# A unit's preparation queued behind the last unit's fourth inversion step, its inputs in one piece a partition, and other places for the first branch

## The chip, the core and the metric

One Trainium2 chip, one of its cores. The metric is the device time of one execution in microseconds, median over several runs. The core's engines run side by side, each in the order of its own instruction queue: TensorE (matrix products and transposes; "PE" in the profile, its weight loads "PEld"), VectorE ("DVE"), ScalarE ("ACT"), GpSimd ("POOL") and SyncE ("SP"), which here issues all data transfers (DMA) between the chip's DRAM and the on-chip memories. SBUF is the working memory with 128 partitions, PSUM the eight banks into which TensorE writes.

## The reference

One layer of a hybrid encoder on x (1024 tokens, 1024 channels), in float32:

```
h = x @ w_in                            # split into inputs of four branches
y_a = rglru(...)                        # linear recurrence with a short convolution
y_b = short_conv(...)                   # gated convolution over 3 tokens
y_c = rwkv7(...)                        # 8 heads of 64, a state of 64 x 64 per head
y_d = chunk_attention(q, k, v, bias)    # 8 heads, chunks of 64, band of 9 chunks
merged = sum over n of sigmoid(x @ w_gate[n] + b_gate[n]) * (y[n] @ w_branch[n])
x = layer_norm(ALPHA * x + merged @ w_out)
ff = square(relu(x @ w_ff1)) @ w_ff2
out = layer_norm(ALPHA * x + ff + (p @ w_ple) * sigmoid(x @ w_ple_gate + b))
```

The step of rwkv7, for each head and token: `sa = state @ a_t`, then `state = state * w_t + sa b_t^T + v_t k_t^T`, then `o_t = state @ r_t`, followed by a normalisation over the head, a bonus term and a gate.

## The kernel before

**Dense products.** A float32 product is made of three products of rounded parts (lines 362 to 364: high x high, high x low, low x high). Pairs of weight columns go through `seven`, a scheme with seven block products instead of eight; x stands on the chip for it as seven blocks, `11`, `21`, `N2`, `N1`, `T3`, `22`, `N4`, each as high and low parts of 512 columns (pool `xp`). A pair uses them in just this order. Results that a later stage needs go to DRAM. A piece is one of the seven products, 12 matmuls of 512 columns.

**Units of the third branch.** The class `Rwkv` handles the recurrence in sixteen units: two halves of the heads (`hf`), eight blocks of 128 tokens (`b`). Counted here from 0 to 15. A unit has these stages:

- Loads by SyncE: `zt` (lines 110 and 111: r, k, v and the two transformed low-rank terms, ten rows of 128 values a partition), `gg` (the gate), `vs` twice (v with its chunks exchanged). `zs` in DRAM holds them, written by `zc_done` (line 626) and `low_rank` (line 686) in pieces of 512 tokens.
- Preparation: ScalarE makes the decays from `zt` (lines 123 and 124), VectorE the running products (lines 128 to 132), the norm of `kk` goes through TensorE (line 147), then `ar`, `bk`, the matrix products of line 191, masked in line 195, transposes (lines 203 and 208) and, last, `YT` in line 221.
- Inversion of a triangular matrix by six doubling steps, `li` 0 to 5: `Yo` (line 237), a product (line 242), an addition (line 243), four transposes (line 227) and a copy by ScalarE (line 228). It ends with a correction (lines 248 to 255) and `TTf` (line 257). `mark` is the last matmul of line 255.
- The tail: two chunks one after the other through the state (lines 261 to 285), normalisation, and the store `ys` (line 308).

Many tiles have one place (`bk`, `wm`, `kk`, `km`, `I`), others two (`zt`, `gg`, `vs`, `ar`, `D`). Five of a unit's intermediate products share the two PSUM banks of tag `q`.

**Order.** Each engine's queue is set at build time by a planner that simulates the engines and takes, whenever one is free, the ready instruction that ranks first. Units are traced with `tc.high_priority(HP)`, HP = 3000, ahead of the dense pieces. After each unit the program traces ten pieces (twelve for the first four units), and from the fourth unit on these may come on TensorE only behind the `mark` of the unit two before (`tc.issue_after`, lines 755 to 758). What `issue_after` names is an instruction; all that the block traces on that instruction's engine is queued behind it.

**After the units.** The other dense pieces (the last are gate products), the attention and the recurrence and convolution branches (`lru`, `sconv`) run side by side (lines 993 to 999). Then `xp`, the temporaries `tx` and the weight buffers `wq` are closed (line 1003), and new pools take their space, in the order in which they are opened: `wfp`, `bp`, `tp`, `lt`. A tile of them waits for those old tiles that lay in its place. The branches are projected in the order 2, 1, 0, 3 (third branch first): four inputs `yf` are loaded and split into `yh` and `yl` (lines 1034 to 1039), at the places that `kind` names, `s1` and `s2` in `bp`, `s3` and `s4` in `lt`; then come the products `br` and the sums `acc` (`s3`).

Of the kernel before, what the change touches and what calls it, by code (L numbers as in the profile page):

```python
# [10 lines left out]
F32 = mybir.dt.float32  # L11
# [30 lines left out]

class Rwkv:


# [33 lines left out]
    def start_half(s, hf):  # L81
        for t in s.P:
            s.nc.gpsimd.memset(t, 0.0)
        s.ip = 0

    def unit(s, hf, b):
        nc, cst, ident = s.nc, s.cst, s.ident
        V, A, G, T, SY = nc.vector, nc.scalar, nc.gpsimd, nc.tensor, nc.sync
        u = f"_{hf}_{b}"
# [15 lines left out]
        def heads(x):  # L105
            return x.rearrange("p (h n) -> p h n", h=4)
# [1 line left out]

        tok = slice(b * 128, b * 128 + 128)
        zt = st("zt", [128, 10, 128])  # L110
        SY.dma_start(zt, s.zs[hf, 0:10, :, tok].rearrange("t p n -> p t n"))
        gg = st("gg", [128, 2, 128])
        SY.dma_start(gg, s.zs[hf, 10:12, :, tok].rearrange("t p n -> p t n"))
        vs = st("vs", [128, 2, 2, 64])
        for c in range(2):
            SY.dma_start(vs[:, :, 1 - c, :], s.zs[hf, 4:6, :, b * 128 + c * 64:b * 128 + c * 64 + 64].rearrange("t p n -> p t n"))
        r, k, v = zt[:, 0:2, :], zt[:, 2:4, :], zt[:, 4:6, :]


        tw = zt[:, 6:8, :].rearrange("p a (c n) -> p (a c) n", c=2)  # L120
# [103 lines left out]
        def transposed(dst, src, n):  # L224
            p = ps("pt")
            for h in range(4):
                T.transpose(p[:, h * 128:h * 128 + 128], src.bitcast(F32)[:, h, :], ident)  # L227
            A.activation(dst, heads(p), AF.Copy)  # L228

        transposed(Y, YT, 0)  # L230
        for li in range(6):
            z = 2 ** li
            n = 64 // z
            Yo = st("Yo", [128, 256], dt=F32R)
            yv = Y.rearrange("p h (n two s) -> p h n two s", two=2, s=z)[:, :, :, 0, :]
            lm = cst[:, C_LV + li * 64:C_LV + li * 64 + 64].rearrange("p (n s) -> p n s", s=z)[:, None].to_broadcast((128, 4, n, z))
            V.tensor_tensor(Yo.rearrange("p (h n s) -> p h n s", h=4, s=z), yv.bitcast(F32), lm, op=ALU.mult)
            if li == 5:
                V.tensor_tensor(Y, Y.bitcast(F32), ident[:, None, :].to_broadcast((128, 4, 128)), op=ALU.add)
            p1 = ps("py", 256)  # L240
            for h in range(4):
                T.matmul(p1[:, h * 64:(h + 1) * 64], YT[:, h, :], Yo[:, h * 64:(h + 1) * 64], start=True, stop=True)  # L242
            V.tensor_tensor(yv, yv.bitcast(F32), p1.rearrange("p (h n s) -> p h n s", h=4, s=z), op=ALU.add)  # L243
            YT = st("YT", [128, 4, 128], dt=F32R)
            transposed(YT, Y, 1 + li)
        Tn, TN = Y, YT
        pr = ps("py")
        T.matmul(heads(pr), s.idr, s.idr[:, None, :].to_broadcast((128, 4, 128)), start=True, stop=False)
# [119 lines left out]
def trunk(ctx, tc, xT, xn, pT, w_in, w_gate, w_branch, w_out, w_ff1, w_ff2, w_ple, w_pg,  # L368
# [25 lines left out]
        turn[tag] = turn.get(tag, -1) + 1  # L394
        return bank(banks[tag][turn[tag] % len(banks[tag])], name, w)

    zs = dr.tile([2, 12, 128, 1024], F32, name="zs")
    zw = dr.tile([128, 1024], F32, name="zw")
    qkv = dr.tile([3, 4, 128, 1024], F32, name="qkv")
    hd = dr.tile([20, 128, 1024], F32, name="hd")  # L400
# [118 lines left out]
    def part(name, k, which, dt=F32R, tile_name=None):  # L519
        return xp.tile([128, 512], dt, tag=f"x{name}{which}{k}", name=tile_name or f"x{name}{which}{k}")  # L520

    def xload(kb, j, k, t):
        SY.dma_start(t, xT[4 * kb + k][:, j * 512:j * 512 + 512])
        return t
# [81 lines left out]
    def xpair(w0, w1, name, done):  # L606

        nx[0] += 1
        return seven(XA, weights(w0, w1, name), name, done, tmp, nx[0] % 2, 1 - nx[0] % 2, late=False)

    def zc_done(i0, keep):

        ds, last = {}, {}

        def finish(i, j):
            t, d = i0 + i, ds.pop((i, j))
            if j:
                V.scalar_tensor_tensor(d[:, 0:1], last[i], mu[:, 0, t:t + 1], d[:, 0:1], op0=ALU.mult, op1=ALU.add)
            if t == 12:
                A.activation(d[0:64, :], d[0:64, :], AF.Tanh)  # L620
                SY.dma_start(zw[:, H[j]], d)
            elif t == 13:
                A.activation(d, d, AF.Tanh, scale=0.5)
                V.tensor_scalar(d, d, 0.5, 0.5, op0=ALU.mult, op1=ALU.add)
            else:
                SY.dma_start(zs[t % 4 // 2, t // 4 * 2 + t % 2][:, H[j]], d)

        def done(i, j, z, sign):
            t = i0 + i
            if sign:  # L630
                p, z = z, keep(f"z{t}{j}")
                A.activation(z, p, AF.Copy, scale=float(sign))
            if t == 13:
                sg.insert(j, rw("zt", "sg1", shape=(128, 1280))[:, 0:512] if j else rw("wm", "sg0"))
            ds[i, j] = d = sg[j and -1] if t == 13 else keep(f"zd{t}{j}")
            A.activation(d, z, AF.Copy, scale=mu[:, 1, t:t + 1])
            V.scalar_tensor_tensor(d[:, 1:512], z[:, 0:511], mu[:, 0, t:t + 1], d[:, 1:512], op0=ALU.mult, op1=ALU.add)
            if j == 0:
                last[i] = mx.tile([128, 1], F32, tag="zl", name=f"zl{t}", bufs=8)
                A.activation(last[i], z[:, 511:512], AF.Copy)  # L640
                finish(i, 0)
            if (i, 1) in ds and i in last:
                finish(i, 1)

        return done
# [6 lines left out]
    def low_rank(d):  # L652


        for kind in range(3):
# [9 lines left out]
            for h in range(2):  # L665
# [9 lines left out]
                for j in range(4):  # L675
                    cs = slice(j * 128, j * 128 + 128)
                    p = ps("q", f"gl{kind}{j}{h}")
                    t = rw("TTf" if j % 2 else "bh", f"lt{kind}{j}{h}", F32)
                    if kind < 2:
                        T.matmul(p, wh[:, cs], dh, start=True, stop=False)  # L680
                        T.matmul(p, wh[:, cs], dl, start=False, stop=True)
                        A.activation(t, p, AF.Tanh, scale=0.5, bias=hb[:, kind, j:j + 1])
                    else:
                        gm.acc(p, [(wh[:, cs], wl[:, cs], dh, dl)])
                        A.activation(t, p, AF.Copy)
                    SY.dma_start(zs[j // 2, 6 + 2 * kind + j % 2][:, sl], t)

    def to_dram(where):

# [60 lines left out]
    for hf in range(2):  # L750
        R.start_half(hf)
        for b in range(8):
            with tc.high_priority(HP):
                marks.append(R.unit(hf, b))
            with ExitStack() as after:
                if len(marks) > max(LAG, L0):
                    after.enter_context(tc.issue_after(marks[-1 - LAG]))
                run(NO if len(marks) > N0 else NOB)
# [245 lines left out]
    banks["g"] = [0, 1]  # L1004
    wf_ = ctx.enter_context(tc.tile_pool(name="wfp", bufs=2, reuse_waits="tile"))
    gm.wf = wf_
    bp = ctx.enter_context(tc.tile_pool(name="bp", bufs=1, reuse_waits="tile"))
    tp = ctx.enter_context(tc.tile_pool(name="tp", bufs=4, reuse_waits="tile"))
    lt = ctx.enter_context(tc.tile_pool(name="lt", bufs=1, reuse_waits="tile"))
    pools = {"s1": bp, "s2": bp, "s3": lt, "s4": lt}  # L1010

# [14 lines left out]
    for n in (2, 1, 0, 3):  # L1026
# [6 lines left out]
        for k in range(4):  # L1033
            yf = wf_.tile([128, 1024], F32, tag="wf", name=f"yf{n}{k}", bufs=2)
            SY.dma_start(yf, ysd[n][k])
            kind = ("s2", "s1", "s4", "s4")[n]
            yh = slot(kind, 2 * k, [128, 1024], F32R, f"yh{n}{k}")
            yl = slot(kind, 2 * k + 1, [128, 1024], F32R, f"yl{n}{k}")
            gm.split(yf, yh, yl)
# [341 lines left out]
```

## Time and profile before

| | |
|---|---|
| three runs, us | 2447.42, 2448.84, 2454.46 |
| median, us | 2448.84 |
| the profiled execution, us | 2449.66 |
| its span (first to last instruction), us | 2447.9 |
| mean granted TensorE clock, share of full speed | 0.96 |

The profile is of one execution. Its span is shorter than its time by what lies before the first and behind the last instruction. The clock of TensorE is granted at one of two levels, 2.4 GHz (1.00) or 1.2 GHz (0.50); a stretch that has both shows a mean. A matmul's busy time includes its pipeline, so a busy TensorE is not one at its peak.

### The profile page before, as it was taken

The numbers are of one execution on the slowest core, as the hardware profiler recorded it, in microseconds if no ns is written. First come the engines' busy times: TensorE is split into PE (matmuls) and PEld (weight loads), VectorE is DVE, ScalarE is ACT, GpSimd is POOL, SyncE is SP. The second block draws the span as 40 slices with busy tenths as digits, with TensorE's granted clock in tenths as the row PEclk, the third lists the DMA queues.
The fourth block names the chain that finished last, engine by engine and source line by source line (L and its number), as shares of the span: only waits on it lengthen the run. The fifth ranks groups of instructions, "written<-read, shape, count | busy, mean of one in ns | idle before, by whom it ended". The sixth has DMA issues, their size and how long they took to land.

```text
span 2447.9 us, 32202 instructions
## 1 busy us (share of the span) xinstructions
PE 2343.9 (96%) x11646; PEld 1912.2 (78%) x11646; DVE 1600.9 (65%) x3183; ACT 1003.3 (41%) x1770; POOL 137.2 (6%) x167
## 2 busy tenths in 40 slices
PE   8999999999999999999968998998999999999998
PEld 6778778777777888878756887886888888888886
DVE  7766766666666666579576455868654444776667
ACT  6653333333333444356665333325355555321110
POOL 1000100000000000000000131000000000000001
PEclk9999999999998999999976999999999999999999
DMA  5362222222222222254344553511123233542311
GB/s 177 128 205 86 77 87 73 74 78 69 83 91 61 78 68 85 91 180 164 118 160 130 159 169 118 181 48 56 44 95 112 103 109 135 180 128 86 103 52 69
DMA packets 152654, 263.85 MB, mean 108 GB/s; under 512 B 23216, under 2 KB 55088, under 8 KB 152496
## 3 DMA queue, kind: packets, MB, share of 16 engines
q1 hardware_dynamic: 152496, 261.81, 32.9%
q8 instruction: 91, 1.49, 0.3%
q14 instruction: 67, 0.55, 0.1%
HBM read 185.73 MB, written 76.02 MB: 107 GB/s over the span
## 4 chain that ended last, share of the span: by engine, by line
PE 82%; DMA 6%; DVE 6%; ACT 3%; issue 2%; SPq 0%; POOL 0%; DVEq 0%; ACTq 0%; POOLq 0%
PE f L364 5%; PE f L363 5%; PE f L362 5%; PE af L364 2%; PE af L362 2%; PE af L363 2%; PE br L362 2%; PE agt L362 2%; PE br L364 2%; PE agt L363 2%; PE br L363 2%; DMA zt<-zs 2%; PE agt L364 2%; PE pt L227 2%; PE po L940 2%
## 5 line engine op out<-in xcount | busy, mean ns | idle before, releaser
L1297 DVE TENSOR_TENSOR x<-x,f 128x512 f32<-128x512 f32 x240 | 159.4, 684 | 75.5 <-PE f L364 74.9
L364 PE MATMUL f<-w2h,a2l 128*128 128x512 f32 x512 | 201.8, 394 | 0.0
L363 PE MATMUL f<-w2l,a2h 128*128 128x512 f32 x512 | 200.9, 392 | 0.0
L362 PE MATMUL f<-w2h,a2h 128*128 128x512 f32 x512 | 198.2, 391 | 0.0
L362 PE MATMUL br<-yh,whwb 128*128 128x512 f32 x256 | 105.9, 414 | 8.9 <-ACT whwb L342 8.0
L363 PEld LDWEIGHTS f<-w2l,a2h 128*128 128x128 f32 x512 | 96.0, 188 | 22.5
L362 PEld LDWEIGHTS f<-w2h,a2h 128*128 128x128 f32 x512 | 96.3, 188 | 21.6
L364 PEld LDWEIGHTS f<-w2h,a2l 128*128 128x128 f32 x512 | 96.1, 188 | 21.2
L343 DVE TENSOR_TENSOR wlf<-wff,whf 128x512 fp32r<-128x512 f32 x96 | 66.1, 688 | 62.6 <-ACT whf L342 62.5
L342 ACT ACTIVATE a2h<-a2f 128x1024 fp32r<-128x1024 f32 x32 | 33.9, 1061 | 173.7 <-PE f L363 110.2
L364 PE MATMUL br<-yh,wlwb 128*128 128x512 f32 x256 | 102.9, 403 | 0.0
L363 PE MATMUL br<-yl,whwb 128*128 128x512 f32 x256 | 102.8, 402 | 0.0
L342 ACT ACTIVATE whf<-wff 128x512 fp32r<-128x512 f32 x96 | 60.6, 631 | 99.0 <-PE af L363 35.6
L228 ACT ACTIVATE YT<-pt 128x512 fp32r<-128x512 f32 x96 | 57.3, 596 | 78.8 <-PE pt L227 78.4
L940 PEld LDWEIGHTS po<-vt,PT 128*128 128x128 f32 x480 | 71.7, 217 | 17.7 <-ACT yd L949 4.7
L940 PE MATMUL po<-vt,PT 128*128 128x64 f32 x480 | 72.7, 296 | 10.5 <-ACT yd L949 4.3
L242 PEld LDWEIGHTS py<-Yo,YT 128*128 128x128 f32 x384 | 59.7, 210 | 14.1 <-ACT YT L228 7.6
L242 PE MATMUL py<-Yo,YT 128*128 128x64 f32 x384 | 63.7, 291 | 5.0 <-ACT YT L228 2.9
L227 PE MATMUL pt<-ident,Y 128*128 128x128 f32 x384 | 66.5, 303 | 0.5 <-DVE Y L243 0.4
L1095 POOL TENSOR_TENSOR mvn<-mvn,nh 128x1 f32<-128x1 f32 x16 | 14.8, 928 | 929.7 <-DVE mvn L1094 929.7
L362 PEld LDWEIGHTS br<-yh,whwb 128*128 128x128 f32 x256 | 49.5, 193 | 20.0 <-ACT whwb L342 8.4
L925 ACT ACTIVATE S<-S,sm 128x640 f32<-128x640 f32 (+2 forms) x64 | 44.2, 691 | 43.0 <-DVE sm L921 31.6
(698 smaller groups left out, 6645.7 us busy)
## 6 DMA issues: line engine op xcount, KB each, us to landing
tl<-gsd SPq DMA_DIRECT2D x64, 256.0 KB, 2.8
wff<-w_ff SPq DMA_DIRECT2D x32, 512.0 KB, 3.9
a2f<-actd SPq DMA_DIRECT2D x32, 512.0 KB, 3.2
w2f<-w_ff SPq DMA_DIRECT2D x32, 512.0 KB, 3.6
zt<-zs SPq DMA_DIRECT2D x16, 640.0 KB, 5.2
qk<-qkv SPq DMA_DIRECT2D x64, 128.0 KB, 2.9
yf<-ys SPq DMA_DIRECT2D x16, 512.0 KB, 3.8
wfwb<-w_branch SPq DMA_DIRECT2D x32, 256.0 KB, 2.8
```

The lines of the kernel that those rows point to most:

```text
L227: T.transpose(p[:, h * 128:h * 128 + 128], src.bitcast(F32)[:, h, :], ident)
L228: A.activation(dst, heads(p), AF.Copy)
L242: T.matmul(p1[:, h * 64:(h + 1) * 64], YT[:, h, :], Yo[:, h * 64:(h + 1) * 64], start=True, stop=True)
L342: s.nc.scalar.activation(hi, src, AF.Copy)
L343: s.nc.vector.tensor_tensor(lo, src, hi.bitcast(F32), op=ALU.subtract)
L362: mm(ps, lh, rh, start=first and i == 0, stop=False, **kw)
L363: mm(ps, lh, rl, start=False, stop=False, **kw)
L364: mm(ps, ll, rh, start=False, stop=last and i == n - 1, **kw)
L925: A.activation(S[:, 0:n], S[:, 0:n], AF.Exp, bias=sm[:, 2:3], accum_out=sm[:, 3:4])
L940: T.matmul(po[:, 0:64], PT[:, c * 128:c * 128 + 128], vt[:, (k0 + c) * 128 + par * 64:(k0 + c) * 128 + par * 64 + 64], start=c == 0, stop= ...
L1095: G.tensor_tensor(mv[:, 3:4], mv[:, 2:3], nh[:, 0:1], op=ALU.pow)
L1297: V.tensor_tensor(x1[i][:, sl], x1[i][:, sl], p, op=ALU.add)
```

## The change

Three edits stand in one diff.

1. The gate. Each unit keeps three instructions of its fourth inversion step (`li == GATE`, GATE = 3): the last matmul of line 242, the addition of line 243 and the ScalarE copy in `transposed`. In the next unit everything that follows the four loads is traced behind them, each on its engine. This holds for the whole rest of the unit, and across the two halves.
2. The layout of `zs`. It was `[half][row][partition][token]`; it becomes `[half][block][partition][row][128 tokens]`. A unit's `zt` is then 5,120 consecutive bytes a partition instead of ten runs of 512, `gg` 1,024 instead of two of 512; `vs` keeps runs of 256. The writes, of 512 tokens, go through the new `to_units` and have four runs of 512 bytes a partition instead of one of 2,048.
3. The places. The parts of the seven blocks are named once in advance, so that they lie in `xp` in the order `11`, `21`, `N2`, `N1`, `T3`, `22`, `N4`. `tp` is opened ahead of `bp`. The first projected branch (n = 2) takes `s1` instead of `s4`, the second (n = 1) `s2` instead of `s1`, the third (n = 0) `s1` instead of `s2`.

```diff
+GATE = 3
...
+        s.gate = getattr(s, "gate", [])
...
-    def unit(s, hf, b):
+    def unit(s, tc, hf, b):
+        with ExitStack() as after:
+            return s.work(tc, after, hf, b)
+
+    def work(s, tc, after, hf, b):
...
-        SY.dma_start(zt, s.zs[hf, 0:10, :, tok].rearrange("t p n -> p t n"))
+        SY.dma_start(zt, s.zs[hf, b, :, 0:10, :])
...
-        SY.dma_start(gg, s.zs[hf, 10:12, :, tok].rearrange("t p n -> p t n"))
+        SY.dma_start(gg, s.zs[hf, b, :, 10:12, :])
...
-            SY.dma_start(vs[:, :, 1 - c, :], s.zs[hf, 4:6, :, b * 128 + c * 64:b * 128 + c * 64 + 64].rearrange("t p n -> p t n"))
+            SY.dma_start(vs[:, :, 1 - c, :], s.zs[hf, b, :, 4:6, c * 64:c * 64 + 64])
         r, k, v = zt[:, 0:2, :], zt[:, 2:4, :], zt[:, 4:6, :]
+        for ins in s.gate:
+            after.enter_context(tc.issue_after(ins))
...
-            A.activation(dst, heads(p), AF.Copy)
+            return A.activation(dst, heads(p), AF.Copy)
...
-                T.matmul(p1[:, h * 64:(h + 1) * 64], YT[:, h, :], Yo[:, h * 64:(h + 1) * 64], start=True, stop=True)
-            V.tensor_tensor(yv, yv.bitcast(F32), p1.rearrange("p (h n s) -> p h n s", h=4, s=z), op=ALU.add)
+                it = T.matmul(p1[:, h * 64:(h + 1) * 64], YT[:, h, :], Yo[:, h * 64:(h + 1) * 64], start=True, stop=True)
+            iv = V.tensor_tensor(yv, yv.bitcast(F32), p1.rearrange("p (h n s) -> p h n s", h=4, s=z), op=ALU.add)
             YT = st("YT", [128, 4, 128], dt=F32R)
-            transposed(YT, Y, 1 + li)
+            ia = transposed(YT, Y, 1 + li)
+            if li == GATE:
+                s.gate = [i.ins for i in (it, iv, ia)]
...
-    zs = dr.tile([2, 12, 128, 1024], F32, name="zs")
+    zs = dr.tile([2, 8, 128, 12, 128], F32, name="zs")
...
+    for n in ("11", "21", "N2", "N1", "T3", "22", "N4"):
+        for k in range(4):
+            part(n, k, "h"), part(n, k, "l")
...
+    def to_units(hf, n, j, t):
+
+        SY.dma_start(zs[hf, 4 * j:4 * j + 4, :, n, :].rearrange("b p n -> p b n"), t.rearrange("p (b n) -> p b n", b=4))
...
-                SY.dma_start(zs[t % 4 // 2, t // 4 * 2 + t % 2][:, H[j]], d)
+                to_units(t % 4 // 2, t // 4 * 2 + t % 2, j, d)
...
-                    SY.dma_start(zs[j // 2, 6 + 2 * kind + j % 2][:, sl], t)
+                    to_units(j // 2, 6 + 2 * kind + j % 2, h, t)
...
-                marks.append(R.unit(hf, b))
+                marks.append(R.unit(tc, hf, b))
...
+    tp = ctx.enter_context(tc.tile_pool(name="tp", bufs=4, reuse_waits="tile"))
     bp = ctx.enter_context(tc.tile_pool(name="bp", bufs=1, reuse_waits="tile"))
-    tp = ctx.enter_context(tc.tile_pool(name="tp", bufs=4, reuse_waits="tile"))
...
-            kind = ("s2", "s1", "s4", "s4")[n]
+            kind = ("s1", "s2", "s1", "s4")[n]
```

## Rows read from the trace of the kernel before

**Rows 1.** the page's head and part 1: busy us, share of the span, instructions.
```profile
span 2447.9 us, 32202 instructions
...
PE 2343.9 (96%) x11646; PEld 1912.2 (78%) x11646; DVE 1600.9 (65%) x3183; ACT 1003.3 (41%) x1770; POOL 137.2 (6%) x167
```

**Rows 2.** busy time by stage: stretch, its length, each engine (instructions), clock, DMA, GB/s.
```profile
141.00:1052.00 911.00, 880.62 (x4956) 717.99 (x4955) 595.57 (x1331) 341.61 (x650) 67.34 (x97) 0.95 0.27 84
861.10:937.00 75.90, 75.65 (x436) 60.54 (x435) 52.99 (x120) 30.58 (x56) 7.80 (x12) 1.00 0.23 75
1210.00:1335.00 125.00, 92.73 (x449) 75.10 (x448) 92.24 (x229) 79.69 (x146) 0.40 (x4) 0.74 0.46 154
1250.00:1280.00 30.00, 17.45 (x74) 14.85 (x74) 25.02 (x47) 17.57 (x31) 0.20 (x2) 0.55 0.47 162
1295.00:1330.00 35.00, 29.47 (x115) 25.88 (x116) 25.56 (x66) 23.33 (x44) 0.00 (x0) 0.50 0.36 112
```

**Rows 3.** line 124, what its engine sat idle for (us, times).
```profile
  DMA zt<-zs: 25.5, 13
```

**Rows 4.** timeline, SyncE, ScalarE and TensorE: start, us, instruction, [idle before <- releaser].
```profile
619.69 0.36 SPq L111 DMA_DIRECT2D zt<-zs  x1
...
625.48 0.51 ACT L124 ACTIVATE inv<-zt,cb 128x256 f32<-128x256 f32 x1 [2.22 <-DMA zt<-zs]
626.37 0.59 ACT L228 ACTIVATE YT<-pt 128x512 fp32r<-128x512 f32 x1
...
627.01 0.51 PE L248 MATMUL py<-idr 128*128 128x512 f32 x1 [2.16 <-ACT YT L228]
```

**Rows 5.** busy time just behind the wait, columns as above.
```profile
630.00:632.00 2.00, 2.00 (x7) 1.61 (x7) 1.56 (x5) 0.00 (x0) 0.00 (x0) 0.50 0.00 0
```

**Rows 6.** timeline, VectorE, line 257 (units 3, 12, 13); all issues of the load.
```profile
363.80 0.69 DVE L257 TENSOR_TENSOR TTf<-p,YT 128x512 f32<-128x512 f32 x1
...
847.73 0.69 DVE L257 TENSOR_TENSOR TTf<-p,YT 128x512 f32<-128x512 f32 x1
...
894.02 0.68 DVE L257 TENSOR_TENSOR TTf<-p,YT 128x512 f32<-128x512 f32 x1
...
L111 SPq DMA_DIRECT2D zt<-zs x16: 359/378/473, 135.9 to 835.4; - x16
```

**Rows 7.** timeline around a fourth step; line 221, first and last start.
```profile
645.20 0.50 ACT L123 ACTIVATE dec<-zt,cb 128x256 f32<-128x256 f32 x1
...
676.17 0.68 DVE L221 TENSOR_TENSOR YT<-AA,cst 128x512 fp32r<-128x512 f32 x1
...
710.49 0.60 ACT L228 ACTIVATE YT<-pt 128x512 fp32r<-128x512 f32 x1 [1.40 <-PE pt L227]
...
L221 DVE TENSOR_TENSOR YT<-AA,cst x16: 673/682/685, 193.3 to 937.0; 128x512 fp32r<-128x512 f32 x16
```

**Rows 8.** first of 28 preparation instructions; eight line 237 steps, first, last.
```profile
L128 DVE TENSOR_TENSOR en<-dec,inv x16: 399/419/426, 144.6 to 865.3; 128x256 f32<-128x256 f32 x16
...
222.06 0.43 DVE L237 TENSOR_TENSOR Yo<-Y,cst 128x256 fp32r<-128x256 f32 x1
...
235.90 0.42 DVE L237 TENSOR_TENSOR Yo<-Y,cst 128x256 fp32r<-128x256 f32 x1
```

**Rows 9.** timeline, the first projected branch: load, split, product.
```profile
1223.79 1.16 SPq L1035 DMA_DIRECT2D yf<-ys  x2
...
1310.37 1.99 ACT L342 ACTIVATE yh<-yf 128x1024 fp32r<-128x1024 f32 x2
...
1323.01 0.79 PE L362 MATMUL br<-yh,whwb 128*128 128x512 f32 x1 [0.45 <-ACT whwb L342]
```

**Rows 10.** DMA issues of one transfer each: count, KB, median us to landing.
```profile
zt<-zs SPq DMA_DIRECT2D x16, 640.0 KB, 5.2
...
zs<-zd SPq DMA_DIRECT2D x24, 256.0 KB, 2.7
...
gg<-zs SPq DMA_DIRECT2D x16, 128.0 KB, 3.2
```

## The prediction

> **What bounds the kernel now.** I read the page's busy shares first: TensorE works in 96% of the span, so time can be won only where it waits or runs at its lower clock level [rows 1]. Next the busy time by stage. Between 141 and 1052 us, where the sixteen units of the third branch run among dense products, TensorE waits 30.4 us and the mean granted clock is 0.95. Between 1210 and 1335 us it waits 32.3 us at a clock of 0.74. These are the two stretches that the change touches [rows 2].
>
> In the first stretch the chain of waits shows a unit's load `zt` on the path again and again. Line 124, ScalarE's first reader of `zt`, waits for the transfer 13 times, 25.5 us in sum [rows 3]. At 619.69 us SyncE issues a `zt`; the unit's line 124 gets it at 625.48 after 2.22 us of idling. The line 228 copies that end one inversion and begin another stand behind it on ScalarE; the second runs at 626.37, and TensorE has waited 2.16 us for it when it starts at 627.01 [rows 4]. Shortly after that the granted clock is 0.50, the 1.2 GHz level, while TensorE is busy throughout [rows 5]. So one late transfer costs twice: the wait, then dense products at half speed.
>
> What a unit costs without it can be read too. Line 257 ends a unit's inversion. From unit 3 to unit 12 it starts at 363.80 and 847.73, nine spacings of 53.8 us. Units 12 and 13 are 46.3 us apart, and by then the last `zt` has been issued, at 835.4 [rows 6]. The difference, 7.5 us, is the price of the wait per unit.
>
> **The gate.** It adds no instruction. TensorE's, VectorE's and ScalarE's share of a unit's preparation is queued behind the fourth step of the unit before. The four loads on SyncE are not gated, nor is GpSimd, which only follows the gated engines. Today's queue, for units 10 and 11: line 221 of unit 10 (its inversion begins) at 676.17, the copy that ends its fourth step at 710.49, but unit 11's line 124 at 625.48 and its line 123 at 645.20, when unit 10 was itself in preparation [rows 4, 7]. Unit 11's `zt` is the one issued at 619.69 [rows 4]. With the gate its line 124 comes after 710.49, some 91 us behind that issue, against a landing time of 5.2 us [rows 10]. The wait is gone by a wide margin, so up to 7.5 us for each of ten spacings, 75 us, can come back.
>
> The gate's price is the chain it creates: line 221 of a unit, four steps, then the whole preparation of the next up to its line 221. Call its length C. Line 221 runs first at 193.3 and last at 937.0, fifteen spacings, 49.6 us on average [rows 7] (under 53.8, because the first two units start close together, which the gate forbids). So the stage changes by 15 x (C - 49.6).
>
> Bounds of C. Steps: today 34.3 us (676.17 to 710.49). At the fastest the trace shows eight steps of two units side by side from 222.06 to 235.90, 3.5 us a step for each; three spacings and an estimated 8.1 us ahead of the first step and from the last to its copy make 18.6 us [rows 7, 8]. Preparation: VectorE has 28 instructions in it, from line 128 (0.42 us) to line 221 (0.68 us), 11.0 us by their medians [rows 7, 8]; with an estimated 5 us of handing over to ScalarE, TensorE and GpSimd 16 us at least. Today it is stretched over 84.8 us, 645.20 to one spacing of 53.8 behind 676.17. So C lies between 34.6 and 119 us, and TensorE's own work keeps a unit at 46.3 in any case [rows 6]. The preparation I place near its fast end: today's 84.8 us are mostly waiting for what one unit leaves to the next (`bk`, `wm`, the two banks of `q`), and these are free by the fourth step. The steps I place between a third and half of their way from 18.6 to 34.3, 23.8 to 26.5, since the next preparation no longer stands between them on VectorE, and stretch the preparation's 16 us by the same factor, 20.5 to 22.8. That makes C 44.3, under the floor and so 46.3, to 49.3; the middle is 47.8: -27 us. Both ends stay: -50 us at 46.3, and several hundred at today's pace of both parts, which I cut at the first rival.
>
> What is late next: the end of the unit's own inversion waits for nothing new, but dense pieces of a unit are queued behind line 255 of the unit two before. If C grows, these are late on TensorE and the engine is empty.
>
> **The inputs in one piece.** `zt` keeps its 640 KB but is 128 pieces of 5,120 bytes and not 1,280 of 512; `gg` likewise; the 48 writes turn from 128 pieces of 2 KB into 512 of 512 bytes. Today: `zt` 5.2 us, `gg` with 256 pieces 3.2, a write 2.7 [rows 10]. A write with 512 pieces lies between 2.7 and 5.2; by the number of pieces near 3.4. They run ahead of the units and beside the first, under dense products, except the last ahead of the first `zt`: +0.7 us there, and about -1 from the load. Later loads are hidden by the gate's 91 us; were it not there, 1 us of 2.2 a unit would be won. Zero in the sum, 3 us either way in the range.
>
> **The places.** No instruction is added. The first branch to be projected (the third, the units' output) has its first two inputs loaded at 1223.79, but ScalarE splits them only at 1310.37, and its first product runs at 1323.01 [rows 9]. Until then TensorE has only attention. The listed places now follow the order in which the last gate pair leaves them, so the small buffers lie on the first block freed and the split inputs on the second to fourth, not on the last block and the temporaries. What can be won: 32.3 us of waiting, plus half of 17.5 and 29.5 us of busy time at the lower level (0.55 and 0.50), 23 us, together 55 us [rows 2]. Against all of it: the branch also needs VectorE, for eight weight splits and sixteen results of 512 columns (0.69 us by line 257 [rows 6]) and four splits of 1,024, by estimate at twice that, 22 us, where it is already busy for 92 of 125 [rows 2]. And the trace does not say whether the split at 1310.37 waited for a place, or only stood behind the recurrence's work, which ends just there. Bounds 0 and -55; neither is nearer, so I take the middle, -27.
>
> **Sum.** The profiled execution took 2449.7 us (span 2447.9 [rows 1]); the median shown is 2448.8, so no correction. 2449.7 - 27 - 27 = 2395.7, say 2395.
>
> **Rivals.** *The gate's chain is too long.* Preparation and steps, now side by side over three units, follow each other. With the steps at today's 34.3 us and the fastest preparation C is 50.3; with 20 us of preparation it is 54.3, and the stage is 70 us longer; less 27 for the places: 2493. Against it: VectorE is busy for only 596 of 911 us in the stage [rows 2], so the steps should close up. It decides for slower from C = 51.4, where the stage loses the 27. 20%.
>
> *Only one half works.* Either C stays near 49.6 and the places give 27 us: 2422; or the split stood behind other work and the gate alone gives its 27: also 2422. 20% with the next one.
>
> *The low clock stays.* The last unit's chain is still cut by short waits, and these alone might keep the clock down. Then only the waiting comes back, 2.2 of 7.5 us a unit: 2.2/7.5 of 27, 8 us, so 2415 with the places. Against it: from 861 to 937 us, with the same chains but without a waited-for `zt`, the mean granted clock is 1.00 [rows 2]. The Trainium skill ("TensorE: Matmul & The Clock Gate", "A second HAM failure mode: psum-queue depth-cycling") says that frequent very short idle times between groups of matmuls can make the clock swing as well as one long wait. By it the sum would be 2415 instead of 2395; the row just named speaks against it here.
>
> *Nothing measurable.* Gains and the gate's price cancel within 7 us: 8%.
>
> **How the numbers follow.** The forecast has 52%: its own range is 2348 (C at 46.3 and 50 us at the places) to 2430. One half or the clock, 20%, lies at 2405 to 2435. About 7 us, 0.3%, is what a measurement of this kernel tells from no change. So faster 0.72, same 0.08, slower 0.20. For eight in ten I leave out some 6% below 2345 and 13% of the long-chain case above 2465.
>
> **What would show it.** Gate: lines 123 and 124 without any wait for `zt`; line 257 at spacings of 46 to 48 us; a granted clock of 0.98 or more between 250 and 900 us; the last line 221 near 900, not 937. Its price: the time from line 221 to the fourth step's copy, and from there to the next line 221, which should be about 25 and 22. Inputs: `zt` landing in about 4 us, writes in 3 to 3.5. Places: the first `yf` split within 20 us of the last gate product, and less than 15 us of TensorE waiting in the 125 us after it. I am wrong if dense products wait for line 255 of an earlier unit, if spacings exceed 51 us, or if the first branch still starts only when the recurrence has ended.

## The result and the profile after

The changed kernel takes 2522.15 us (median; 2517.23 to 2529.69), the kernel before 2450.47 beside it: a ratio of 1.0294, interval 1.0263 to 1.0325. That is 72 us slower. The forecast was 2395 us, with a range to 2465.

The lines of the changed kernel have moved: 123, 124, 221, 228, 257 are now 133, 134, 231, 238, 269. The page of the changed kernel, against [rows 1]: TensorE is busy for 36 us more, in a span that is 74 us longer.

```profile
span 2521.6 us, 32170 instructions
...
PE 2380.1 (94%) x11646; PEld 1936.0 (77%) x11646; DVE 1609.4 (64%) x3183; ACT 999.0 (40%) x1770; POOL 135.1 (5%) x167
```

Busy time by stage of the changed kernel (columns as in [rows 2]): the units, the rest of the dense products with the attention, the recurrence's last stretch, the first projected branch, the rest.

```profile
141.00:1135.00 994.00, 939.00 (x5075) 761.06 (x5074) 614.43 (x1352) 348.27 (x670) 65.84 (x96) 0.91 0.26 80
...
1135.00:1294.00 159.00, 140.26 (x712) 113.93 (x711) 111.60 (x264) 103.12 (x186) 0.34 (x5) 0.95 0.51 165
1294.00:1410.00 116.00, 90.70 (x440) 74.64 (x440) 85.54 (x228) 70.88 (x136) 0.40 (x4) 0.74 0.38 124
1410.00:1585.00 175.00, 163.60 (x876) 137.85 (x874) 92.58 (x210) 57.96 (x115) 43.11 (x32) 0.99 0.47 152
1585.00:2521.00 936.00, 916.07 (x4016) 746.17 (x4016) 602.25 (x956) 330.94 (x507) 14.83 (x16) 0.99 0.31 100
```

The same view of the kernel before, its last stretch.

```profile
1510.00:2447.00 937.00, 914.96 (x4016) 745.31 (x4016) 602.43 (x956) 330.18 (x507) 14.85 (x16) 0.99 0.30 101
```

The tail is equal, 936 and 937 us. The stage of the units took 911 us before [rows 2] and takes 994 now: 83 us more, at a clock of 0.91 and not 0.95. From its end to the tail it is 450 us where it was 458 (1052 to 1510), which gives 8 back. So the loss is in the units.

Where in the units? Line 231 (a unit's inversion begins) of the changed kernel, units 0, 3, 13 and 15, and line 221 of the kernel before, units 3 and 13 (0 and 15 are in [rows 7]).

```profile
189.15 0.69 DVE L231 TENSOR_TENSOR YT<-AA,cst 128x512 fp32r<-128x512 f32 x1
...
334.08 0.67 DVE L231 TENSOR_TENSOR YT<-AA,cst 128x512 fp32r<-128x512 f32 x1
...
893.39 0.68 DVE L231 TENSOR_TENSOR YT<-AA,cst 128x512 fp32r<-128x512 f32 x1
...
1019.27 0.68 DVE L231 TENSOR_TENSOR YT<-AA,cst 128x512 fp32r<-128x512 f32 x1
```

```profile
306.13 0.68 DVE L221 TENSOR_TENSOR YT<-AA,cst 128x512 fp32r<-128x512 f32 x1
...
837.22 0.68 DVE L221 TENSOR_TENSOR YT<-AA,cst 128x512 fp32r<-128x512 f32 x1
```

Unit 0 to 3: 144.9 us against 112.9, 32 more. Unit 3 to 13, ten spacings: 559.3 against 531.1, 28 more (55.9 a unit against 53.1). Unit 13 to 15: 125.9 against 99.8, 26 more.

And what is in them? From here on an empty stretch is a gap of over 4 us between dense products on TensorE. Counted from the timelines, the stage has thirteen of them in both kernels, 169 us in sum before and 256 us now. That is 87 us more, about what the stage lost. The stage also holds 118 dense matmuls more than before, which were taken forward from behind the units.

**One unit.** ScalarE and VectorE in the changed kernel, from the start of unit 11's inversion to that of unit 12; the copy of line 238 at 822.55 ends the fourth step.

```profile
802.31 0.60 ACT L238 ACTIVATE YT<-pt 128x512 fp32r<-128x512 f32 x1 [1.61 <-PE pt L237]
814.48 0.59 ACT L238 ACTIVATE YT<-pt 128x512 fp32r<-128x512 f32 x1
819.88 0.60 ACT L238 ACTIVATE YT<-pt 128x512 fp32r<-128x512 f32 x1 [0.38 <-PE pt L237]
822.55 0.60 ACT L238 ACTIVATE YT<-pt 128x512 fp32r<-128x512 f32 x1 [2.08 <-PE pt L237]
823.05 0.50 ACT L133 ACTIVATE dec<-zt,cb 128x256 f32<-128x256 f32 x1
```

```profile
785.88 0.68 DVE L231 TENSOR_TENSOR YT<-AA,cst 128x512 fp32r<-128x512 f32 x1
...
842.18 0.67 DVE L231 TENSOR_TENSOR YT<-AA,cst 128x512 fp32r<-128x512 f32 x1
```

The gate works as written: line 133 comes right behind the copy. From 785.88 to 822.55 it is 36.7 us of steps, from 823.05 to 842.18 it is 19.1 us of preparation. Over units 3 to 12 the steps take 37.8 us on average, and from their last copy to the next line 231 it is 18.1. Before, the four steps of unit 10 took 34.3 us, to 710.49 [rows 7], and from there to unit 11's line 221 it was 19.5:

```profile
729.96 0.68 DVE L221 TENSOR_TENSOR YT<-AA,cst 128x512 fp32r<-128x512 f32 x1
```

So in the middle of the stage the same two parts added up to 53.8 us already. The average of 49.6 in the prediction came from the ends of the stage, where units were closer.

Busy time of the changed kernel from one `mark` to the next, cut where the dense products end; below it one such period of the kernel before.

```profile
779.20:817.80 38.60, 38.60 (x228) 31.41 (x228) 21.19 (x44) 14.13 (x28) 1.21 (x3) 1.00 0.25 82
817.80:823.50 5.70, 3.26 (x23) 2.35 (x21) 5.28 (x14) 3.09 (x8) 1.90 (x2) 0.95 0.29 92
823.50:835.80 12.30, 11.02 (x44) 9.10 (x43) 9.37 (x25) 1.97 (x5) 1.21 (x1) 0.50 0.01 2
```

```profile
741.00:781.00 40.00, 40.00 (x238) 32.61 (x239) 29.23 (x66) 15.28 (x30) 4.21 (x6) 1.00 0.20 63
781.00:791.30 10.30, 7.91 (x44) 6.97 (x44) 5.53 (x12) 3.45 (x7) 0.00 (x0) 0.71 0.42 118
```

Here the reader sees the mechanism. Ten dense pieces are released by a mark. While they last, TensorE is busy without a gap, and the steps stand between the pieces in its queue: the copies at 802.31 and 814.48 are 12 us apart, those at 819.88 and 822.55, when the pieces are used up, 2.7. Behind that comes a stretch without dense products, 10.3 us before and 18.0 now. The VectorE work that used to lie beside the dense products (29.2 us) lies to a larger part in the empty stretch (14.7 us, not 5.5): it is the preparation. And in that stretch the granted clock falls to the 1.2 GHz level (0.50 from 822.9 us). TensorE in the empty stretch of the unit before it:

```profile
767.28 0.63 PE L252 MATMUL py<-Yo,YT 128*128 128x64 f32 x4 [0.75 <-ACT YT L238]
768.73 1.12 PE L237 MATMUL pt<-ident,Y 128*128 128x128 f32 x4 [0.81 <-DVE Y L253]
770.59 1.06 PE L252 MATMUL py<-Yo,YT 128*128 128x64 f32 x4 [0.75 <-ACT YT L238]
```

The same four products take 0.63 us at 767.28 and 1.06 at 770.59; in between, from 768.3 us, the granted clock is 0.50, though no engine waits for `zt`.

**The first branch** in the changed kernel: ScalarE's first split, first and last early product on TensorE, the recurrence's last store, the first accumulation.

```profile
1273.98 1.06 ACT L354 ACTIVATE yh<-yf 128x1024 fp32r<-128x1024 f32 x1 [2.85 <-DMA yf<-ys]
...
1292.74 0.78 PE L374 MATMUL br<-yh,whwb 128*128 128x512 f32 x1
...
1300.46 0.39 PE L376 MATMUL br<-yh,wlwb 128*128 128x512 f32 x1
...
1400.89 0.33 SPq L858 DMA_DIRECT2D ys<-y  x1
...
1403.49 1.26 DVE L1074 SCALAR_TENSOR_TENSOR acc<-tl,br 128x512 f32<-128x512 f32 x2
```

The split is free early, 8 us after the last gate product (1265.58), not behind the recurrence as in [rows 9]. But two products fill the two banks of `br`, and the accumulations that would free them come only behind the recurrence's last store. The hold has moved by one step.

### The profile page after: what moved, and what is told of

Its sections match the earlier page's. It is cut to its first block, busy times and chain, and to the rows that moved or that the text cites. A ratio compares the mean times of both kernels' runs of the same rounds, so it can differ in the third digit from the quotient of the medians.

```text
span 2521.6 us, 32170 instructions
## 1 busy us (share of the span) xinstructions
PE 2380.1 (94%) x11646; PEld 1936.0 (77%) x11646; DVE 1609.4 (64%) x3183; ACT 999.0 (40%) x1770; POOL 135.1 (5%) x167
## 4 chain that ended last, share of the span: by engine, by line
PE 82%; DVE 8%; DMA 5%; ACT 3%; issue 2%; SPq 0%; DVEq 0%; ACTq 0%
PE f L376 5%; PE f L375 5%; PE f L374 5%; PE af L376 2%; PE af L374 2%; PE pt L237 2%; PE af L375 2%; PE agt L374 2%; PE pq L201 2%; PE agt L376 2%; PE agt L375 2%; DMA qk<-qkv 2%; PE br L374 2%; PE br L375 2%; PE br L376 2%
## 5 line engine op out<-in xcount | busy, mean ns | idle before, releaser
L376 PEld LDWEIGHTS f<-w2h,a2l 128*128 128x128 f32 x512 | 96.1, 188 | 21.2
L238 ACT ACTIVATE YT<-pt 128x512 fp32r<-128x512 f32 x96 | 57.1, 595 | 128.5 <-PE pt L237 128.1
L355 DVE TENSOR_TENSOR wlf<-wff,whf 128x512 fp32r<-128x512 f32 x96 | 66.1, 688 | 62.0 <-ACT whf L354 61.4
L354 ACT ACTIVATE whf<-wff 128x512 fp32r<-128x512 f32 x96 | 60.6, 631 | 98.5 <-PE af L375 35.5
L237 PE MATMUL pt<-ident,Y 128*128 128x128 f32 x384 | 73.1, 322 | 23.6 <-DVE Y L253 23.5
L252 PE MATMUL py<-Yo,YT 128*128 128x64 f32 x384 | 66.4, 300 | 26.5 <-ACT YT L238 19.5
L237 PEld LDWEIGHTS pt<-ident,Y 128*128 128x128 f32 x384 | 51.9, 163 | 36.1 <-DVE Y L253 28.2
L253 DVE TENSOR_TENSOR Y<-Y,py 128x256 fp32r<-128x256 f32 x96 | 40.1, 418 | 48.4 <-PE py L252 47.3
L374 PEld LDWEIGHTS br<-yh,whwb 128*128 128x128 f32 x256 | 49.2, 192 | 23.1 <-ACT whwb L354 7.9
```

The costliest lines, as they stand in the source:

```text
L238: return A.activation(dst, heads(p), AF.Copy)
L252: it = T.matmul(p1[:, h * 64:(h + 1) * 64], YT[:, h, :], Yo[:, h * 64:(h + 1) * 64], start=True, stop=True)
L253: iv = V.tensor_tensor(yv, yv.bitcast(F32), p1.rearrange("p (h n s) -> p h n s", h=4, s=z), op=ALU.add)
L354: s.nc.scalar.activation(hi, src, AF.Copy)
L355: s.nc.vector.tensor_tensor(lo, src, hi.bitcast(F32), op=ALU.subtract)
L374: mm(ps, lh, rh, start=first and i == 0, stop=False, **kw)
```

## The experiments

Unless said otherwise, a spacing is the mean of the ten from unit 3 to 13. Steps are the time from line 231 to the copy that ends the fourth step.

**Which part.** First the gate alone on the kernel before, and the changed kernel without it (shown).

```diff
-        for ins in s.gate:
-            after.enter_context(tc.issue_after(ins))
```

> The kernel before with the wait behind the fourth inversion step alone; inputs and places as before. Theory 1 (the wait strings four steps and a preparation into one chain of about 37 + 19 = 56 us a unit, against an average of 49.6 before): units about 55 to 57 us apart, the last recurrence store near 1135 us, the whole 2515 to 2540 us. Theory 2 (the loss comes from the new input layout or the moved places): 2430 to 2455 us, units about 50 us apart.

Measured: ratio 1.0283 (1.0237 to 1.0330), 2520.4 us; spacing 55.9 us, last recurrence store of the units at 1137.9.

> The changed kernel without the wait: inputs in one piece a partition and the moved places stay. Theory 1: units about 50 us apart again, the last recurrence store near 1050 us, the whole 2425 to 2450 us (the earlier start of the first branch gives 0 to 25 us). Theory 2: 2500 us or more, as the changed kernel.

Measured: ratio 0.9948 (0.9921 to 0.9974), 2440.45 us; spacing 52.2, last store at 1037.0. The gate alone makes the loss; the other two parts make a small gain. Theory 1 holds, theory 2 falls.

**Inputs and places by themselves**, without the gate, the layout of `zs` in the one, the order of the pools, the parts and `kind` in the other.

> The kernel before with the inputs in one piece a partition alone; no wait behind a step, places as before. The changed kernel without its wait took 2440 us and its last recurrence store came at 1037 us, 15 us earlier than before. Theory 1 (this came from the inputs, which ended the preparation's wait of 2 us a unit): last recurrence store at 1033 to 1042 us, the whole 2432 to 2447 us. Rival (it came from the moved places): last recurrence store near 1050 us, the whole 2448 to 2460 us.

Measured: ratio 0.9964 (0.9939 to 0.9989), 2441.75 us. The whole is as expected, the place is not: the profiled execution has its last store at 1052.0 and still waits for `zt`, though less: the two readers wait 27.9 us in sum, and 35.5 in the kernel before (25.5 of them at line 124 [rows 3]). That execution, with a span of 2447 us, lies near the upper end of its ten runs (2430 to 2449), so where the 9 us arise stays open.

> The kernel before with the moved places alone. Theory 1 (the first branch's products start early, but its second step, the accumulations, stay behind the last recurrent scan of the branch before it, so that four products of sixteen at most run ahead): the whole 2445 to 2460 us, no difference from before that can be measured. Rival (the early start is worth its 25 us): 2420 to 2432 us.

Measured: ratio 1.0001 (0.9980 to 1.0022), 2451.4 us: nothing, as theory 1 has it (two products ran ahead, not four). The first split comes at 1226.5 us in place of 1310.4 [rows 9], so it had waited for its place; the first accumulation comes at 1332.8, behind the recurrence's last store at 1329.7.

**How far behind.** The wait at the second and the third step.

```diff
-GATE = 3
+GATE = 1
```

> The changed kernel with the wait behind the second inversion step in place of the fourth. Theory 1 (only the length of the chain matters): two steps and a preparation are about 18 + 19 = 37 us, under the 50 us that a unit takes anyway, so the wait binds hardly at all: units 49 to 51 us apart, 2425 to 2455 us. Rival (a wait that ties the preparation to the chain costs at any place, since the engines' queues stand behind it): units 53 us apart or more, 2480 us or more.

Measured: ratio 0.9913 (0.9889 to 0.9936), 2432.32 us; spacing 50.5. That is 8 us less than without a wait, and all ten executions (2424.8 to 2434.6) lie below all ten of the changed kernel without it (2435.3 to 2448.9). But the units as a whole are not faster. What the middle spacings gain, the ends give back: unit 0 to 3 takes 123.2 us against 111.5, unit 13 to 15 takes 108.8 against 99.7. The last store, without a wait and then with it:

```profile
L318 SPq DMA_DIRECT2D ys<-y x16: 377/378/393, 257.6 to 1037.0; - x16
```

```profile
L320 SPq DMA_DIRECT2D ys<-y x16: 370/377/392, 259.9 to 1038.8; - x16
```

So the 8 us are gained behind the units; why, no run shows.

```diff
-GATE = 3
+GATE = 2
```

> The changed kernel with the wait behind the third step. Theory 1 (the chain's length against the spacing decides): three steps and a preparation are about 27 + 19 = 46 us, still under 50, so the spacing stays at 49 to 51 us and the whole at 2425 to 2450 us. Rival (the cost grows evenly with the place of the wait, since each step that is put ahead of the preparation takes it out of the dense products' cover): 2465 to 2490 us, half way between the wait behind the second step and behind the fourth.

Measured: ratio 1.0005 (0.9989 to 1.0021), 2452.85 us; spacing 51.1. The spacing is at the end of what was expected, the whole missed its range by 3 us; the rival's even growth is not there either, since 20 us lie between the second and the third step, and 69 between the third and the fourth.

ScalarE's lines for `zt` without a gate (the changed kernel without its wait: lines 131 and 132), then with the wait at the second step (line 133; none at line 134), what the engine sat idle for (us, times):

```profile
  DMA zt<-zs: 5.9, 3
...
  DMA zt<-zs: 20.1, 13
```

```profile
  DMA zt<-zs: 1.1, 1
```

Busy time with the wait at the second step, two dense stretches and the empty one between them:

```profile
723.10:763.40 40.30, 40.30 (x240) 32.80 (x240) 27.57 (x65) 15.34 (x31) 2.57 (x5) 1.00 0.18 59
763.40:773.00 9.60, 7.18 (x53) 5.77 (x51) 7.65 (x17) 3.57 (x7) 1.57 (x2) 1.00 0.52 138
773.00:813.50 40.50, 40.50 (x241) 32.89 (x239) 27.22 (x65) 17.18 (x33) 2.82 (x5) 1.00 0.21 68
```

VectorE's work is back beside the dense products (27.6 us), the wait for `zt` is nearly gone, and the clock is 1.00 throughout. In other empty stretches of that run it still falls, from 818.0 to 824.5 us to 0.50.

**More, fewer and other dense products**, wait at the fourth step throughout.

```diff
-NO = 10
+NO = 14
```

> The changed kernel with 14 pieces of dense products released by each unit's mark in place of 10. Theory 1 (TensorE runs out of released products 17 us before each mark, and the chain sets the spacing): the stretch without dense products shrinks from 17 us to under 8, the spacing stays at 55 to 60 us, the products moved forward are missing behind the units, and the whole falls to 2455 to 2500 us. Rival (TensorE's own work sets the spacing, not the chain): each piece added lengthens the unit by its some 3.8 us, units 65 to 70 us apart, and the whole stays at 2510 to 2530 us.

Measured: ratio 1.0652 (1.0605 to 1.0698), 2609.07 us; spacing 66.1. Theory 1 as stated here falls: the empty stretch shrank only to 13.9 us on average, from 17.5, and the four steps grew from 37.8 to 45.8. The rival's spacing came, its whole did not (79 us over its range). A piece is twelve matmuls, 0.23 us apart, 2.75 us; four pieces made a unit 10.1 us longer. Busy time of this run, dense and empty stretch:

```profile
659.40:711.30 51.90, 51.90 (x292) 42.02 (x292) 27.87 (x58) 17.66 (x35) 4.07 (x7) 1.00 0.30 97
711.30:725.60 14.30, 10.75 (x48) 8.84 (x46) 11.73 (x31) 3.44 (x7) 1.21 (x1) 0.68 0.05 18
```

The added pieces do not go into the empty stretch. They go into the steps. The units' last store comes at 1230.3, 95 us later than in the changed kernel, and the whole loses 87 of them.

```diff
-NO = 10
+NO = 8
```

> The changed kernel, its wait behind the fourth step as it is, with 8 pieces of dense products released by each mark in place of 10. Theory 1 as the run with 14 pieces left it (the released pieces run inside the four steps and stretch them by their own 2.75 us each; behind the wait TensorE has none): steps near 31 us in place of 36.5, units 50 to 52 us apart, the stretch without dense products still 16 to 20 us, last recurrence store 1065 to 1085 us; the pieces put off fill the attention's gaps or lengthen it, the whole 2490 to 2530 us. Rival (the chain takes its 56 us whatever is put in it): units 55 to 56 us apart, the whole over 2525 us.

Measured: ratio 1.0131 (1.0076 to 1.0187), 2482.4 us; spacing 51.3, steps 31 to 37 us, empty stretch 19.8, last store at 1078.2. Theory 1 in its new form holds, but for the whole, which is 8 us better than its range: the units end 57 us earlier than in the changed kernel, and what follows them grows by only 17.

Then the ten pieces as they were, four of them queued behind the same fourth step:

```diff
+NL = 4
...
+            gate = R.gate
...
+            late = NL if len(marks) > N0 else 0
...
-                run(NO if len(marks) > N0 else NOB)
+                run((NO if len(marks) > N0 else NOB) - late)
+            if late:
+                with tc.issue_after(gate[0]):
+                    run(late)
```

> The changed kernel, wait behind the fourth step, 10 pieces a unit as before, but 4 of the 10 are queued behind the same fourth step on TensorE, so that they run beside the next preparation in place of inside the steps. Theory 1 (the loss is that the preparation and the last two steps run without dense products): steps down from 36.5 to 25 to 28 us, the stretch without dense products down from 17 to under 10, units 47 to 52 us apart, the whole 2425 to 2465 us. Rival (the wait costs by the length of its chain of dependent operations, with or without dense products beside it): units over 54 us apart, the whole over 2500 us.

Measured: ratio 1.0275 (1.0234 to 1.0316), 2522.22 us; spacing 55.0. None of theory 1's numbers came, both of the rival's did. But the kernel does not do all that was meant. One period of this run: steps, empty, late pieces, empty.

```profile
385.20:412.10 26.90, 26.90 (x159) 22.56 (x159) 13.90 (x26) 8.21 (x17) 0.20 (x2) 0.92 0.18 57
412.10:417.10 5.00, 4.09 (x34) 3.31 (x32) 3.44 (x10) 2.51 (x5) 0.49 (x1) 0.96 0.25 83
417.10:431.60 14.50, 14.50 (x66) 11.70 (x66) 10.44 (x25) 5.29 (x12) 2.43 (x3) 0.90 0.24 73
431.60:444.10 12.50, 9.37 (x46) 7.89 (x46) 8.75 (x22) 1.64 (x3) 1.21 (x1) 0.72 0.24 75
```

The fourth step's last product and its copy in the same period:

```profile
416.43 0.81 PE L252 MATMUL py<-Yo,YT 128*128 128x64 f32 x4 [0.16 <-ACT YT L238]
...
424.37 0.58 ACT L238 ACTIVATE YT<-pt 128x512 fp32r<-128x512 f32 x1
```

The late pieces hang on that product, and ScalarE's preparation on that copy. Between the two, 21 to 23 of the late pieces' 48 matmuls stand on TensorE, ahead of the step's own transposes. So up to the product the steps did fall, from 36.2 to 29.0 us on average, but the copy comes 7.1 us behind it and no longer 1.6. Half of what was to run beside the preparation ran inside the fourth step again. The empty stretch is only cut in two, 17.0 us in sum on average against 17.5. What late pieces behind the copy would do is not shown.

Over the four kernels with the wait at the fourth step, the spacing less 2.75 us a piece is 27.6 (14 pieces), 28.4 (10), 27.5 (10, split) and 29.3 (8); before the change it is 25.6, with the wait at the second step 23.0. So a piece cost a unit about its own time in both places that were tried, ahead of the fourth step's last product and right behind it.

**The ends of the stage.** Only the preparations of units 4 to 13 wait.

```diff
-        for ins in s.gate:
+        for ins in s.gate if 4 <= 8 * hf + b <= 13 else ():
```

> The changed kernel, wait behind the fourth step, but only for the preparations of units 4 to 13; units 1 to 3 and 14 and 15 prepare freely. Theory (of the 83 us by which the last recurrence store came later, 32 arose from unit 0 to unit 3 and 26 from unit 13 to unit 15, where dense products are not rationed by a mark and stretch the steps to 45 us ahead of the waiting preparation; 28 arose in between): unit 3 near 306 us, units 4 to 13 some 56 us apart, unit 15 near 965, last recurrence store at 1070 to 1090 us, the whole 2455 to 2480 us. Rival (each waiting preparation costs the same 83 / 15 = 5.5 us): the whole 2490 to 2505 us.

Measured: ratio 1.0093 (1.0076 to 1.0110), 2474.84 us; unit 3 at 303.0, units 4 to 13 57.1 us apart, unit 15 at 972.5, last store at 1084.5. The theory holds. Two thirds of the loss (0.0201 of 0.0294) come from the five preparations at the ends. There, by the order in which the program traces them, the dense products of the first units, and those that follow the last unit's, hang on no mark. In line with it, the steps of units 2, 14 and 15 took 46 to 49 us with 8, 10 and 14 pieces a mark alike.

**The first branch's hold.** The accumulators in a pool of their own, wait at the second step. The second branch's operands (`s2`) get a pool of their own too.

```diff
-GATE = 3
+GATE = 1
...
+    at = ctx.enter_context(tc.tile_pool(name="at", bufs=1, reuse_waits="tile"))
+    b2p = ctx.enter_context(tc.tile_pool(name="b2p", bufs=1, reuse_waits="tile"))
     lt = ctx.enter_context(tc.tile_pool(name="lt", bufs=1, reuse_waits="tile"))
-    pools = {"s1": bp, "s2": bp, "s3": lt, "s4": lt}
+    pools = {"s1": bp, "s2": b2p, "s3": at, "s4": lt}
...
-        wl = bp.tile([128, 1024], F32R, tag=f"s2_{k}", name=f"{name}l{k}")
+        wl = b2p.tile([128, 1024], F32R, tag=f"s2_{k}", name=f"{name}l{k}")
```

> The wait behind the second step, and the accumulators of the first branch in a pool of their own over operand blocks alone, so that they no longer share a pool with tiles that lie over the recurrent branch's buffers; the second branch's operands move behind them. In the changed kernel the first accumulation came at 1403.5 us, right behind the last recurrent store at 1400.9. Theory 1 (the pool held the accumulations, and TensorE lacked products meanwhile): accumulations start over 50 us ahead of the last recurrent store, and the whole falls by 15 to 40 us against the same kernel with the shared pool (2432 us), to 2392 to 2417. Rival (attention and the scans set the end of that stretch, and products taken forward are missing as cover later): accumulations early as well, the whole 2425 to 2440 us.

Measured: ratio 0.9806 (0.9771 to 0.9841), 2404.34 us, 28 us less than with the shared pool. Accumulations and the recurrence's four last stores in this run, first and last start; then the stretch in which the recurrence ends:

```profile
L1076 DVE SCALAR_TENSOR_TENSOR acc<-tl,br x16: 661/682/689, 1232.4 to 1291.0; 128x512 f32<-128x512 f32 x16
```

```profile
L858 SPq DMA_DIRECT2D ys<-y x4: 332/434/535, 1103.9 to 1315.3; - x4
```

```profile
1290.00:1400.00 110.00, 98.74 (x518) 83.00 (x517) 73.17 (x167) 51.38 (x99) 27.85 (x20) 0.91 0.50 154
```

All sixteen accumulations are done before the recurrence ends, 83 us ahead for the first. Theory 1 holds: the division into pools held the accumulations. By the tile sizes in the code the accumulators' own tiles lay over operand blocks in the changed kernel too, and shared only the pool with tiles over the recurrence's buffers; the traces show no addresses, so this part is argued. This is the best version here, and it beats both kernels.

> The kernel with the accumulators in a pool of their own, without any wait behind a step. The same kernel with the wait behind the second step took 2404 us. If the light wait's 8 us (2432 against 2440 with the shared pool) are its own and add up: 2408 to 2418 us. Rival (they were the chance of one order): within 4 us of 2404.

Measured: ratio 0.9850 (0.9810 to 0.9890), 2417.55 us. This is inside the first range, and the rival falls. With the wait at the second step it is 13 us less, with the shared pool 8 us less (2432.32 against 2440.45). The wait gains in both pairs, and in neither do the executions overlap.

## Why the prediction was wrong

**Failed: "the steps I place between a third and half of their way from 18.6 to 34.3, 23.8 to 26.5, since the next preparation no longer stands between them on VectorE".** They took 36.7 us in the unit shown and 37.8 on average. VectorE was not what held them: it is busy for 21.2 of 38.6 us in that stretch, TensorE for all of it. The steps stand in TensorE's queue between ten dense pieces; with 14 pieces they took 45.8 us, with 8 some 31 to 37. The prediction argued from VectorE's load over the whole stage and never looked at TensorE's queue between two steps. Its fast end hid the same thing: the 3.5 us a step were read from 222 to 236 us, inside a stretch without dense products (223.91 to 251.49), and the 8.1 and 5 us that it calls estimates come from no row.

**Nearly right: the preparation.** 19.1 us in the unit shown, a little under the 20.5 to 22.8 named.

**Right as a formula, wrong in its C.** Fifteen spacings by (C - 49.6): with the mean spacing of 55.3 (189.1 to 1019.3 over 15) it gives 86 us, and the last store of the units is 83 us later. The rival with the too long chain named the longer chain, though not what makes it long, with C = 54.3, a point of no return at 51.4, and 2493 us; it was given 20%. It was short by 29 us. The stage lost 83 and not 70, as unit 2 to 3 and 14 to 15 took 65 and 70 us. And what follows the units gave back 8 and not 27: the places alone gave nothing (1.0001), and with the gate alone the time from the units' last store to the end fell as well, from 1396 to 1380 us. (The lower end of the forecast's own range, 2348, is 2350 by its own terms, which changes nothing.)

**Failed: 7.5 us a unit as the price of the wait for `zt`.** The wait vanished, as forecast: 0.3 us at line 133, none at line 134. But where only the wait goes and the chain stays short (second step), the spacing falls from 52.2 to 50.5 us in the middle, 1.7 a unit, and over all fifteen it does not fall at all (48.9 and 49.2). The late spacing of 46.3 in [rows 6] had another cause, which no run isolates, and as a floor it was too low: the shortest mean spacing from unit 3 to 13 is 50.5.

**The rival on the clock.** In the stage the clock went down, not up, 0.95 to 0.91. Its mechanism shows in the empty stretches, where waits of 0.5 to 0.8 us between groups precede the fall to 0.50 at 768.3 us. The Trainium skill ("TensorE: Matmul & The Clock Gate", "A second HAM failure mode: psum-queue depth-cycling") describes, for another kernel, a clock that swings because of frequent short idle times between groups. The trace agrees in part: here 1.06 us in place of 0.63 for the same products, but from 763.4 to 773.0 us of the run with the wait at the second step there are waits of 0.7 and 0.9 us as well, and the clock stays at 1.00. It is not the first cause: the stretch has to be empty first. By the mean clocks of the stretches, 171 us of the stage are at the lower level, all but 7 of them in empty stretches. Before it was 96, of which 25 lay in the dense ones. So what the prediction wanted, dense products at full clock, came, and it was worth little.

**Inputs.** The landing was right; the DMA issues of the changed kernel, against [rows 10]:

```profile
zt<-zs SPq DMA_DIRECT2D x16, 640.0 KB, 3.9
...
zs<-zd SPq DMA_DIRECT2D x24, 256.0 KB, 3.0
...
gg<-zs SPq DMA_DIRECT2D x16, 128.0 KB, 2.4
```

Zero in the sum could not be seen beside the gate. For the case without a gate the prediction named 1 us of the wait a unit; alone the layout is worth 0.4%, 9 us, and the wait is 7.6 us shorter in sum, which fits in size.

**Places.** Whether the split at 1310.37 waited for a place is answered: it did, since with the places alone it comes 84 us earlier, and in the changed kernel 8 us after the last gate product. "Less than 15 us of TensorE waiting in the 125 us after it" failed, 39 us of the 125 behind 1265.6 remain, and 25 of the 116 from 1294 to 1410. The step that failed is to have asked what holds the split and not what holds the next one behind it.

What stays open: why the spacing less the pieces' own time is nearly constant under the gate, 27.5 to 29.3 us. That the planner spends released pieces on the first operations it can put them beside, and that the next mark hangs on what is left, fits all runs but is argued, not shown.

## What to carry to other kernels

When work is queued behind a link of another chain, both become one chain, and its length must be taken from the trace with the filler beside it: here the fillers, not the engine that the moved work used, set how long the steps took. Place such a wait at the earliest link that does the job; behind the second step it took the input wait away and the whole was 8 us shorter than without it, behind the fourth it was 82 us longer. And take the spacing at the ends too: an average over a chain's middle and its ends fits neither. Where a place is freed early and the time does not move, look at the next instruction in the line: it may hang on its pool's neighbours and not on its own place.

## What the runs showed of the hardware that was not expected

From 763 to 768 us TensorE had no wait longer than 0.9 us between its groups, and the granted clock still fell to the 1.2 GHz level at 768.3. Over the dense stretches of the stage it was 0.93 to 1.00, so that almost only the chain's own small products paid for it: 0.63 us became 1.06. Writes of 512-byte pieces in place of 2,048 took 3.0 us and not 2.7, with four times the pieces; the forecast of 3 to 3.5 held.
